# Cached forget gates loaded 64 keys to a partition and summed there, their sums stored once, in a hybrid encoder step on one core

## The chip, the cores and the metric

The kernel runs on one core of a Trainium2 chip. The metric is the time of one execution on the device, in microseconds (us); the time of a kernel is the median of its runs. The engines are called as in the profile: PE is TensorE's matmul, PEld its weight load, DVE is VectorE, ACT is ScalarE, POOL is GpSimd, SP is SyncE, which in this kernel issues every DMA.

## What is computed

One inference step of a trunk of one layer. 1024 frames of a new stream (the prompt) and 16 new frames of each of 8 running streams (the decode rows; each has 1024 past keys in a cache) go through the same layer: RMSNorm, one input projection, three groups of token mixers side by side (stick-breaking attention "sb", a state-space group "ssd", forgetting attention "fox"; 4 heads of 64 in each attention group), one output projection, cross-attention and a SwiGLU FFN. The change concerns the forgetting attention. Its scores have a bias made of running sums of log forget gates:

```python
logf = jax.nn.log_sigmoid((fg + p['fox_b_f']).astype(jnp.float32))   # new rows, 4 heads
...
# prompt: fcum = jnp.cumsum(logf, axis=1)
# decode rows, for each stream:
fcum = jnp.cumsum(jnp.concatenate([past['fox_logf'].astype(jnp.float32), logf], axis=1), axis=1)
fox_o = fox_attend(fq, fox_k, fox_v, fcum[:, past_len:], fcum, qpos, kpos)

def fox_attend(q, k, v, fq, fk, q_pos, k_pos):
    s = jnp.einsum('bqhd,bkhd->bhqk', q, k).astype(jnp.float32) * (HEAD_DIM ** -0.5)
    s = s + (fq[..., :, None] - fk[..., None, :])          # heads moved to the front
    valid = k_pos[None, :] <= q_pos[:, None]
    p = jax.nn.softmax(jnp.where(valid, s, -jnp.inf), axis=-1)
    return jnp.einsum('bhqk,bkhd->bqhd', p, v.astype(jnp.float32))
```

`past['fox_logf']` is the input `cache_fox_logf` with the shape [1, 8 streams, 1024 keys, 4 heads]: 8192 rows of four floats, 0.13 MB. The new `logf` are outputs too (`p_fox_logf` of the prompt, `s_fox_logf` of the decode rows).

## The kernel before

Large products are fp32 in three fp32r products: each operand is split into a high part (`wh`, cast by ACT at L290) and a low part (`wl`, the rest, subtracted at L132 on POOL or DVE), and L326, L327, L328 multiply high by high, low by high and high by low. Tiles come from pools whose names the profile shows: `psd`, `pss`, `pst`, `pso` are PSUM banks for dense products, scores, transposes and outputs of attention; `wr` is a raw piece of a weight or of a cache, `wh` and `wl` its two parts; `ws` a row of scores or weights, `xc` a wide row, `sg` and `so` small scratch tiles, `act` and `st` larger ones, `vr` raw cached values.

The order of the instructions on each engine is set by a scheduler that simulates the program, so the position in the code is a priority, not a place. SP carries all DMAs in one queue of instructions; an SP instruction whose buffer is not free yet stops those behind it.

After the first projections the program is one long pipeline. It steps through units of attention, first those of the sb group, then those of the fox group, and after each unit's step takes one step of a generator of dense work, `fill_s()`: the projections of the fox group's q, k and v, then `fox_sums()`, then z0, dt, xbc and z1, then the ssd group. A prompt unit computes scores of 128 queries (L559, L560, with a mask at L562), turns them into a row of weights (for sb: sigmoids L516 and L517 on ACT and a scan over the row, L519, on DVE; for fox: the bias L529 on ACT, then the exponential) and later multiplies the row by v after transposing it (L577, L592). A decode unit `p` (of four in each group) treats 128 query rows at once, 2 streams of 4 heads of 16 rows. Its cached keys are loaded (L882, two streams by two halves of 512 keys, each in two pieces), transposed on PE (L888, result to PSUM `pst`), multiplied (L873); its weights are multiplied by a reversed product on POOL (L132), transposed on PE (L925) and multiplied by cached values loaded at L943. In the fox group, ACT first writes the bias of all 1024 past keys at L529 from a tile `fkb` that holds, for each of the 128 rows, the 1024 sums of its stream and head (`xc<-fssc`, loaded at L909), and from `fqs`, the sum at the query's own position (loaded at L1246).

`fox_sums()` (L658 to L727) makes these sums. It stores the new gates (L662, L663), loads the cached ones (L666), and builds two masks on POOL: `triu`, a triangle of ones, and `ones`. The prompt's sums are a triangle product and a product with ones (L678, L679) over blocks of 128 rows, transposed (L690) and stored to DRAM as `fcsc` (L692). The cached gates come 128 keys to a column:

```python
SP.dma_start(out=pl0[:, :256].rearrange("p (u h) -> p u h", h=4),
             in_=a["cache_fox_logf"][0].rearrange("b k h -> (b k) h").rearrange("(u p) h -> p u h", p=P))
```

so that partition `p` holds key `p` of each of 64 blocks. They are regrouped (L683), the sums of whole blocks are added up on DVE (L693, L696), and fifteen products on PE (L708 with the triangle, L710 with ones) give 32 rows (8 streams by 4 heads) of 1024 sums in PSUM, copied by ACT. The 16 new rows of each stream follow with a product by `fold` (L713), a scan (L716) and the addition of the last past sum. All of it goes to DRAM twice, `fssc[32, 2, 1040]`, and L909 reads from there, for a unit `p`, 8 rows in 2 copies, each 8 times, in one DMA of 128 partitions.

Of the kernel before, what the change touches and what calls it, by code (L numbers as in the profile page):

```python
# [17 lines left out]
P = 128  # L18
# [3 lines left out]
DEC_B = 8  # L22
# [40 lines left out]
def tile_hybrid_step(ctx: ExitStack, tc: tile.TileContext, a: dict):  # L63
# [37 lines left out]
    def sg_t(dt=F32):  # L101
        return sgp.tile([P, 512], dt, tag="sg", name="sg")
# [128 lines left out]
    def dram(shape, dt, name):  # L231
        return dr.tile(shape, dt, name=name, tag=name)
# [8 lines left out]
    fs_sc = dram([32, 2, PAST + DEC_S], F32, "fssc")  # L241
# [416 lines left out]
    def fox_sums():  # L658
# [6 lines left out]
        pl0, pl1 = sg_t(), sg_t()  # L665
        SP.dma_start(out=pl0[:, :256].rearrange("p (u h) -> p u h", h=4),  # L666
                     in_=a["cache_fox_logf"][0].rearrange("b k h -> (b k) h").rearrange("(u p) h -> p u h", p=P))
        triu, ones = pl1[:, 256:384], pl1[:, 384:512]
        POOL.memset(pl1[:, 256:], 1.0)
# [11 lines left out]

        pp, ps_ = pl1[:, :256], pl0[:, 256:]
        DVE.tensor_copy(pp.rearrange("p (k b h) -> p k b h", k=8, h=4),  # L683
                        pl0[:, :256].rearrange("p (b k h) -> p k b h", k=8, h=4))
# [8 lines left out]
        DVE.tensor_copy(ps_[:, 32:64], pp[:, 0:32])  # L693
# [3 lines left out]
        x8 = sg2_t()  # L697
        DVE.tensor_tensor(out=x8[:, :32].rearrange("p (b h) -> p b h", h=4),
                          in0=lf[:, 8, :].unsqueeze(1).to_broadcast([P, 8, 4]),
                          in1=smask.unsqueeze(2).to_broadcast([P, 8, 4]), op=ALU.mult)  # L700
        yield

        sr = xc_t()[0:32, :PAST + DEC_S]
        for hf in range(2):
            tp = pd()
            for k in range(4 * hf, 4 * hf + 4):
                o = tp[:32, (k % 4) * P:(k % 4 + 1) * P]
                PE.matmul(o, pp[:, k * 32:(k + 1) * 32], triu, start=True, stop=k == 0)  # L708
# [1318 lines left out]
```

## Time and profile before

| | |
|---|---|
| runs | 1922.89, 1914.52, 1916.93 us; median 1916.93 |
| profiled execution | 1915.89 us, its span 1914.2 us |
| busy share of the span | PE 96%, PEld 86%, DVE 47%, ACT 43%, POOL 33% |
| DMA | 305.70 MB in 309742 packets, mean 160 GB/s |
| mean granted TensorE clock | 0.988 |

How to read the lines that follow. A row of windows gives a stretch, its length, then for PE, PEld, DVE, ACT and POOL the busy time with the number of instructions that start in it, the granted TensorE clock as a part of full speed, the mean busy share of the 16 DMA engines (it can pass 1 where transfers overlap on an engine) and the rate in GB/s. A row of the timeline gives the start, the duration, the engine (SPq: SP's queue), line, operation, output and input with their shapes and a count, and in brackets the idle time before it with what ended it. A row of waits gives the waiting engine, tile and line, what it waited for, the total, the number and the longest. Numbers behind tile names are left out there.

### The profile page before, as it was taken

To read this page: it belongs to the slowest core of one execution; us is meant where nothing else is said; L and a number is where in the kernel's file an instruction comes from. 1 tells how busy PE (TensorE), PEld (TensorE's weight loads), DVE (VectorE), ACT (ScalarE), POOL (GpSimd) and SP (SyncE) were. 2 spreads that over 40 slices of the span, in tenths; PEclk is the share of its full clock that TensorE was granted. 3 is DMA by queue.
4 is the path that set the end of the run, shared out by engine and by line. 5 is a ranking of instruction groups with operands and counts; after the bars stand their busy time and mean duration, and the time that the engine had idled before them with its cause. 6 is when DMAs were issued, how large, how long until landed. Compare 5 with 4: busy or idle time off the path is not lost. (4 is left out here: it accounts for less than half of the span.)

```text
span 1914.2 us, 32508 instructions
## 1 busy us (share of the span) xinstructions
PE 1837.6 (96%) x12146; PEld 1641.4 (86%) x12146; DVE 897.1 (47%) x1823; ACT 823.7 (43%) x1782; POOL 622.6 (33%) x921
## 2 busy tenths in 40 slices
PE   7989989999998889999999999999999999999998
PEld 5889877888876667898998889999999999888886
DVE  3421323457646873353445387333333433455554
ACT  6431534545566771243433275333333333344443
POOL 7532416254324563211102205544444443000000
PEclk9999998999999999999999999999999999999999
DMA  9455645536579887244558124322323223567572
GB/s 336 142 165 159 211 115 152 154 109 185 166 220 282 280 290 260 103 150 145 176 194 291 66 91 111 80 70 70 95 74 75 70 70 100 190 194 237 177 246 92
DMA packets 309742, 305.70 MB, mean 160 GB/s; under 512 B 89996, under 2 KB 261108, under 8 KB 309584
## 3 DMA queue, kind: packets, MB, share of 16 engines
q1 hardware_dynamic: 309584, 303.62, 51.6%
q8 instruction: 96, 1.57, 0.3%
q14 instruction: 62, 0.51, 0.1%
HBM read 229.31 MB, written 74.24 MB: 159 GB/s over the span
## 5 line engine op out<-in xcount | busy, mean ns | idle before, releaser
L132 POOL TENSOR_TENSOR wl<-wr,wh 128x256 fp32r<-128x256 f32 (+2 forms) x184 | 138.6, 787 | 222.4 <-ACT wh L290 202.0
L326 PE MATMUL psd<-act,wh 128*128 128x384 f32 x576 | 198.7, 345 | 5.1 <-DVE sg L453 2.7
L327 PE MATMUL psd<-act,wh 128*128 128x384 f32 x576 | 197.6, 343 | 0.0
L328 PE MATMUL psd<-act,wl 128*128 128x384 f32 x576 | 196.8, 342 | 0.7 <-POOL wl L132 0.7
L1849 PE MATMUL pst<-bT,tr 128*128 128x256 f32 (+1 forms) x1068 | 155.0, 293 | 0.0
L1849 PEld LDWEIGHTS pst<-bT,tr 128*128 128x128 f32 x1068 | 144.9, 188 | 0.1
L328 PE MATMUL psd<-wh,act 128*128 128x512 f32 (+3 forms) x424 | 135.8, 322 | 0.0
L326 PE MATMUL psd<-wh,act 128*128 128x256 f32 (+3 forms) x414 | 133.0, 324 | 2.4 <-ACT pt L1445 1.2
L1849 PE MATMUL psd<-bT,tr 128*128 128x320 f32 (+1 forms) x912 | 133.2, 295 | 0.8 <-DVE tr L1693 0.5
L327 PE MATMUL psd<-wl,act 128*128 128x256 f32 (+3 forms) x414 | 132.8, 322 | 0.5 <-POOL wl L132 0.5
L1849 PEld LDWEIGHTS psd<-bT,tr 128*128 128x128 f32 x912 | 124.7, 188 | 1.8 <-DVE tr L1693 0.7
L326 PEld LDWEIGHTS psd<-act,wh 128*128 128x128 f32 x576 | 109.1, 189 | 8.7 <-DVE sg L453 3.1
L132 POOL TENSOR_TENSOR tr<-u,tr 128x256 fp32r<-128x256 f32 x110 | 81.9, 774 | 102.3 <-ACT tr L1689 85.1
L328 PEld LDWEIGHTS psd<-act,wl 128*128 128x128 f32 x576 | 108.9, 189 | 2.3 <-POOL wl L132 1.0
L327 PEld LDWEIGHTS psd<-act,wh 128*128 128x128 f32 x576 | 109.0, 189 | 1.5 <-issue 1.1
L132 POOL TENSOR_TENSOR ws<-ws 128x256 f32<-128x256 f32 (+2 forms) x100 | 68.5, 713 | 115.3 <-DVE ws L519 99.9
L1824 DVE TENSOR_TENSOR tr<-tr,pst 128x256 f32<-128x256 f32 (+1 forms) x86 | 38.6, 449 | 139.5 <-ACT tr L1821 106.3
L251 POOL TENSOR_SCALAR sm<-sm 128x1 f32<-128x1 f32 (+2 forms) x27 | 7.1, 261 | 296.6 <-ACT y L1932 208.0
L132 POOL TENSOR_TENSOR tr<-raw,tr 128x256 fp32r<-128x256 f32 x94 | 69.2, 765 | 84.5 <-ACT tr L1689 76.3
L1689 ACT CAST tr<-tr 128x384 fp32r<-128x384 f32 (+1 forms) x70 | 37.7, 538 | 121.1 <-DMA tr<-hidsc 104.3
L290 ACT CAST wh<-wr 128x512 fp32r<-128x512 f32 (+2 forms) x90 | 52.2, 621 | 80.7 <-PE psd L328 31.0
L326 PEld LDWEIGHTS psd<-wh,act 128*128 128x128 f32 x414 | 78.3, 189 | 9.9 <-ACT pt L1445 1.5
(620 smaller groups left out, 4714.0 us busy)
## 6 DMA issues: line engine op xcount, KB each, us to landing
u<-w_down SPq DMA_DIRECT2D x40, 512.0 KB
raw<-w_down SPq DMA_DIRECT2D x26, 512.0 KB
st<-qksc SPq DMA_DIRECT2D x48, 256.0 KB
wr<-w_in SPq DMA_DIRECT2D x44, 256.0 KB
tr<-hidsc SPq DMA_DIRECT2D x57, 192.0 KB
hidsc<-tr SPq DMA_DIRECT2D x34, 288.0 KB
qksc<-sg SPq DMA_DIRECT2D x48, 192.0 KB
wr<-cache_sb_k SPq DMA_DIRECT2D x32, 256.0 KB
```

Of the source, the lines that this page charges most:

```text
L132: POOL.tensor_tensor(out=out[:, a0:a1], in0=in0[:, a0:a1], in1=in1[:, a0:a1], op=op)
L251: POOL.tensor_scalar(v, ss, inv, EPS, ALU.mult, ALU.add)
L290: ACT.copy(hi, raw)
L326: PE.matmul(out, ah, bh, start=start, stop=False)
L327: PE.matmul(out, ah, bl, start=False, stop=False)
L328: PE.matmul(out, al, bh, start=False, stop=stop)
L1689: ACT.copy(hi, src)
L1824: DVE.tensor_tensor(out=at(out, g), in0=at(x, g), in1=ps[g][:, :GW[g]], op=op)
L1849: PE.matmul(dst[g][:, :GW[g]], x[:, ka], y[:, k, :], start=start and k == 0 and m == 0, stop=stop and k == 3 and m == 2, skip_group_check= ...
```

## The change

The cached gates are loaded as they lie in memory: 64 keys of a stream, each with 4 heads, make 1 KB, and 128 partitions take the 8192 keys (partition = stream x 16 + chunk of 64 keys). On each partition four scans on DVE (one for each head, stride 4 in, dense out) make the running sums of the 64 keys. The last sum of each chunk (`tot`) goes through one product with a mask `before` (ones where the chunk belongs to the same stream and comes earlier), and the result, one number for each partition and head, is added to the 64 sums. The fifteen products and the sums of blocks are gone. The totals of the streams come from a product of `t8` with a column of ones (L710), and are added to the scan of the new rows. The sums are stored once, `fssc[4 heads, 8 streams, 1024]` (L719), the new rows' sums apart in `fnsc[32, 16]` (L721). A unit's `fkb` tile is now loaded by two DMAs (L913), one for each of its two streams: 64 partitions, 4 rows of 1024 sums, each 16 times. `fqs` is loaded from `fnsc` (L1249).

```diff
-    fs_sc = dram([32, 2, PAST + DEC_S], F32, "fssc")
+    fs_sc = dram([4, DEC_B, PAST], F32, "fssc")
+    fn_sc = dram([32, DEC_S], F32, "fnsc")
...
-        pl0, pl1 = sg_t(), sg_t()
-        SP.dma_start(out=pl0[:, :256].rearrange("p (u h) -> p u h", h=4),
-                     in_=a["cache_fox_logf"][0].rearrange("b k h -> (b k) h").rearrange("(u p) h -> p u h", p=P))
-        triu, ones = pl1[:, 256:384], pl1[:, 384:512]
+        lp, tri = sg_t(), sg_t()
+        SP.dma_start(out=lp[:, :256], in_=a["cache_fox_logf"][0].rearrange("b (c k) h -> (b c) (k h)", k=64))
+        triu, ones, before = (tri[:, i * P:(i + 1) * P] for i in range(3))
...
+        b3 = before.rearrange("p (b t) -> p b t", t=16)
+        POOL.affine_select(out=b3, in_=b3, compare_op=ALU.is_ge, fill=0.0, base=-1, pattern=[[16, 8], [1, 16]],
+                           channel_multiplier=-1)
+        POOL.affine_select(out=b3, in_=b3, compare_op=ALU.is_ge, fill=0.0, base=0, pattern=[[-16, 8], [0, 16]],
+                           channel_multiplier=1)
...
-        DVE.tensor_copy(pp.rearrange("p (k b h) -> p k b h", k=8, h=4),
-                        pl0[:, :256].rearrange("p (b k h) -> p k b h", k=8, h=4))
...
-        for k in range(1, 7):
-            sl = slice(32 * k, 32 * k + 32)
-            DVE.tensor_tensor(out=ps_[:, 32 * k + 32:32 * k + 64], in0=ps_[:, sl], in1=pp[:, sl], op=ALU.add)
+        for hd in range(4):
+            x = lp[:, hd:256:4]
+            DVE.tensor_tensor_scan(lp[:, 256 + 64 * hd:320 + 64 * hd], x, x, 0.0, ALU.add, ALU.bypass)
+        tot = pre[:, 32:36]
+        DVE.tensor_copy(tot, lp[:, 319:512:64])
...
-        for hf in range(2):
-            tp = pd()
-            for k in range(4 * hf, 4 * hf + 4):
-                o = tp[:32, (k % 4) * P:(k % 4 + 1) * P]
-                PE.matmul(o, pp[:, k * 32:(k + 1) * 32], triu, start=True, stop=k == 0)
-                if k:
-                    PE.matmul(o, ps_[:, k * 32:(k + 1) * 32], ones, start=False, stop=True)
-            ACT.copy(sr[:, hf * 512:(hf + 1) * 512], tp[:32])
         tp = pd()
-        PE.matmul(tp[:32, :16], x8[:, :32], fold, start=True, stop=True)
+        PE.matmul(tp[:, :4], before, tot, start=True, stop=True)
+        PE.matmul(tp[:32, 16:32], x8, fold, start=True, stop=True)
+        PE.matmul(tp[:32, 32:48], t8, ones[:, :16], start=True, stop=True)
+        DVE.tensor_tensor(out=lp[:, 256:512].rearrange("p (h k) -> p h k", h=4),
+                          in0=lp[:, 256:512].rearrange("p (h k) -> p h k", h=4),
+                          in1=tp[:, 0:4].unsqueeze(2).to_broadcast([P, 4, 64]), op=ALU.add)
...
-        SP.dma_start(out=fs_sc, in_=sr.unsqueeze(1).to_broadcast([32, 2, PAST + DEC_S]))
+        SP.dma_start(out=fs_sc.rearrange("h b (c k) -> (b c) h k", k=64),
+                     in_=lp[:, 256:512].rearrange("p (h k) -> p h k", h=4))
+        SP.dma_start(out=fn_sc, in_=n8)
...
-            SP.dma_start(out=fkb[:, :PAST],
-                         in_=fs_sc[8 * p:8 * p + 8, :, :PAST].rearrange("i c k -> (i c) k").unsqueeze(1)
-                         .to_broadcast([16, DEC_S // 2, PAST]))
+            for b2 in range(2):
+                SP.dma_start(out=fkb[64 * b2:64 * b2 + 64, :PAST],
+                             in_=fs_sc[:, 2 * p + b2, :].unsqueeze(1).to_broadcast([4, DEC_S, PAST]))
```

Line numbers behind the changed function shift by three or four: L882 becomes L885, L888 L891, L909 L913, L925 L928; those ahead of it by one (L315 becomes L316). Only two places of the program are put in another order: the one around `fox_sums`, and the one where `fkb` is loaded.

SP's queue around the load of the cached gates, before. The names are the tile, its number and where the data come from; p_fox_logf and s_fox_logf are the stores of new gates, w_in the weights of the z projection:

```order
L666 DMA sg_2949<-cache_fox_logf 128x64x4
L882 DMA wr_3017<-cache_sb_k 128x512
L882 DMA wr_3019<-cache_sb_k 128x512
L608 DMA mixsc_199<-sg_2921 64x2x256
L882 DMA wr_3034<-cache_sb_k 128x512
L882 DMA wr_3036<-cache_sb_k 128x512
L662 DMA p_fox_logf<-lf_192 128x8x4
L663 DMA s_fox_logf<-lf_192 128x4
L315 DMA wr_3218<-w_in 128x2x256
L315 DMA wr_3218<-w_in 128x2x8
```

SP's queue at the same place, after:

```order
L668 DMA sg_2950<-cache_fox_logf 128x256
L885 DMA wr_3019<-cache_sb_k 128x512
L885 DMA wr_3021<-cache_sb_k 128x512
L609 DMA mixsc_199<-sg_2922 64x2x256
L885 DMA wr_3036<-cache_sb_k 128x512
L885 DMA wr_3038<-cache_sb_k 128x512
L316 DMA wr_3202<-w_in 128x2x256
L316 DMA wr_3202<-w_in 128x2x8
L316 DMA wr_3203<-w_in 128x2x256
L316 DMA wr_3203<-w_in 128x2x8
L316 DMA wr_3218<-w_in 128x2x256
L316 DMA wr_3218<-w_in 128x2x8
```

The order up to the key loads is the same; the two stores of new gates, which stood ahead of the w_in loads, now stand behind six of them.

PE from the first cached keys of this decode unit on, before (L888 transposes keys, L873 multiplies them, L577 transposes weights of a prompt unit, L678 and L679 are the prompt's sums, L690 their transposes):

```order
L873 MATMUL pss<-kf,st 32x512 x4
L888 MATMUL pst<-ident,wr 128x128 x8
L678 MATMUL psd<-lf,sg 128x32
L888 MATMUL pst<-ident,wr 128x128 x4
L679 MATMUL psd<-so,sg 128x28
L888 MATMUL pst<-ident,wr 128x128 x4
L577 MATMUL pst<-ident,ws 128x128 x4
L690 MATMUL psd<-ident,fqc 4x128 x8
L577 MATMUL pst<-ident,ws 128x128 x4
L873 MATMUL pss<-kf,st 32x512 x4
L577 MATMUL pst<-ident,ws 128x128 x3
```

PE at the same place, after:

```order
L876 MATMUL pss<-kf,st 32x512 x4
L891 MATMUL pst<-ident,wr 128x128 x13
L578 MATMUL pst<-ident,ws 128x128 x4
L891 MATMUL pst<-ident,wr 128x128 x3
L578 MATMUL pst<-ident,ws 128x128 x4
L685 MATMUL psd<-lf,sg 128x32
L578 MATMUL pst<-ident,ws 128x128 x3
L876 MATMUL pss<-kf,st 32x512 x4
L904 MATMUL pss<-dm,identr 128x128
L905 MATMUL pss<-st 32x128 x4
L593 MATMUL pso<-pt,st 64x256 x4
L686 MATMUL psd<-so,sg 128x28
```

The triangle product of the prompt's sums (L678, now L685) has moved from the middle of the key transposes to behind them, and the product with ones (L679, now L686) further back still. The join of the chunks stands later on PE, ahead of the first transposes of the decode weights (L925 before, L928 now):

```order
L560 MATMUL pss<-st 128x512
L561 MATMUL pss<-st 128x512
L708 MATMUL psd<-so,sg 128x4
L709 MATMUL psd<-fold,so 32x16
L710 MATMUL psd<-sg,so 32x16
L560 MATMUL pss<-st 128x512
L561 MATMUL pss<-st 128x512
L563 MATMUL pss<-mask_sb,identr 128x128
L928 MATMUL pst<-ident,ws 128x128 x4
```

Here the three small products stand between pieces of 512 keys of a prompt unit, where before the fifteen products with 32 rows stood ahead of such pieces and the product with `fold` alone behind them.

DVE at this place, before (`lf` is the tile of new gates, L402 to L410 compute their logarithm):

```order
L450 TENSOR_TENSOR sg<-so,sg 64x256
L402 TENSOR_SCALAR sg<-sg 128x36
L403 RECIPROCAL sg<-sg 128x36
L404 TENSOR_TENSOR sg<-sg 128x36
L405 TENSOR_TENSOR sg<-sg 128x36
L406 TENSOR_SCALAR sg<-sg 128x36
```

DVE at the same place, after (the scans are listed as SCALAR_TENSOR_TENSOR):

```order
L451 TENSOR_TENSOR sg<-so,sg 64x256
L699 SCALAR_TENSOR_TENSOR sg<-sg 128x64 x4
L403 TENSOR_SCALAR sg<-sg 128x36
L701 COPY so<-sg 128x4
L404 RECIPROCAL sg<-sg 128x36
L704 TENSOR_TENSOR so<-so,smask 128x32
L405 TENSOR_TENSOR sg<-sg 128x36
```

The four scans, which read the loaded gates, now stand ahead of the logarithm of the new gates.

More of the change, by code (lines that the diff above doesn't have):

```diff
@@ L713, in fox_sums @@
-        PE.matmul(tp[:32, :16], x8[:, :32], fold, start=True, stop=True)
-        ACT.copy(x8[0:32, 64:80], tp[:32, :16])
-        n8 = x8[0:32, 64:80]
+        for hd in range(4):
[3 more added lines that the diff above has]
+        DVE.tensor_copy(tot, lp[:, 319:512:64])
+        x8, t8 = pre[:, 64:96], pre[:, 96:128]
+        for out, src in ((x8, lf[:, 8, :]), (t8, tot)):
+            DVE.tensor_tensor(out=out.rearrange("p (b h) -> p b h", h=4), in0=src.unsqueeze(1).to_broadcast([P, 8, 4]),
+                              in1=smask.unsqueeze(2).to_broadcast([P, 8, 4]), op=ALU.mult)
@@ L716, in fox_sums @@
+        n8 = pre[0:32, 128:144]
+        DVE.tensor_copy(n8, tp[:32, 16:32])
         DVE.tensor_tensor_scan(n8, n8, n8, 0.0, ALU.add, ALU.bypass)
[L717 to L718 removed]
+        DVE.tensor_tensor(out=n8, in0=n8, in1=tp[:32, 32:48], op=ALU.add)
+        SP.dma_start(out=fs_sc.rearrange("h b (c k) -> (b c) h k", k=64),
+                     in_=lp[:, 256:512].rearrange("p (h k) -> p h k", h=4))
```

14 lines of the change are left out of this document (3 added, 11 removed).

## The prediction

> **What bounds the kernel now.** I read the page's busy times first, then the busy time of each engine by stretch, then TensorE's waits in the stretch that holds the changed code, then that stretch in order of time.
>
> ```profile
> PE 1837.6 (96%) x12146; PEld 1641.4 (86%) x12146; DVE 897.1 (47%) x1823; ACT 823.7 (43%) x1782; POOL 622.6 (33%) x921
> ```
>
> TensorE is busy for 96% of the span, so a change pays only where it takes TensorE work away or closes one of its gaps. By stretch (columns: stretch, its length, busy time of PE, PEld, DVE, ACT, POOL with instructions, granted TensorE clock, DMA share, GB/s):
>
> ```profile
> 200.00:276.00 76.00, 72.84 (x575) 63.64 (x574) 23.24 (x36) 34.92 (x82) 25.73 (x44) 0.98 0.56 171
> 276.00:312.00 36.00, 25.63 (x167) 20.16 (x166) 14.92 (x43) 19.29 (x45) 19.55 (x31) 0.76 0.75 165
> 312.00:400.00 88.00, 85.94 (x714) 76.25 (x715) 42.91 (x78) 40.16 (x96) 40.51 (x58) 1.00 0.49 141
> ...
> 500.00:600.00 100.00, 93.11 (x707) 77.46 (x706) 56.15 (x176) 58.06 (x131) 22.04 (x40) 0.98 0.80 227
> 600.00:700.00 100.00, 86.60 (x717) 66.86 (x716) 81.43 (x226) 76.32 (x174) 61.91 (x104) 0.97 0.84 266
> ```
>
> The forget-gate sums run from 276 to 312, and there TensorE is idle for 10.4 of 36 us, at a mean clock of 0.76. TensorE's own waits from 250 to 340 (total, times, longest):
>
> ```profile
> PE pst L888 <- DMA wr<-cache_sb_k: 5.5, 3, 4.9
> PE pst L925 <- POOL ws L132: 3.5, 1, 3.5
> ```
>
> The same place in order of time, from two windows:
>
> ```profile
> 276.99 0.45 SPq L666 DMA_DIRECT2D sg<-cache_fox_logf  x1
> 277.54 5.25 SPq L882 DMA_DIRECT2D wr<-cache_sb_k  x2
> 283.56 1.02 SPq L882 DMA_DIRECT2D wr<-cache_sb_k  x2
> 284.20 0.29 DVE L683 COPY sg<-sg 128x256 f32<-128x256 f32 x1 [1.11 <-DMA sg<-cache_fox_logf]
> 285.00 1.51 PE L888 MATMUL pst<-ident,wr 128*128 128x128 f32 x6 [4.91 <-DMA wr<-cache_sb_k]
> ...
> 286.12 5.14 SPq L315 DMA_DIRECT2D wr<-w_in  x8
> 287.52 1.09 PE L888 MATMUL pst<-ident,wr 128*128 128x128 f32 x4 [0.32 <-DMA wr<-cache_sb_k]
> 292.48 0.63 ACT L290 CAST wh<-wr 128x528 fp32r<-128x528 f32 x1 [1.66 <-DMA wr<-w_in]
> 293.20 8.52 POOL L132 TENSOR_TENSOR wl<-wr,wh 128x256 fp32r<-128x256 f32 x12 [9.76 <-PE pst L577]
> 297.77 2.56 DVE L519 TENSOR_TENSOR_SCAN ws<-ws 128x1152 f32<-128x1152 f32 x1 [8.67 <-ACT ws L516]
> 301.72 3.56 POOL L132 TENSOR_TENSOR ws<-ws 128x256 f32<-128x256 f32 x3
> 304.73 0.49 PE L925 MATMUL pst<-ident,ws 128*128 128x128 f32 x1 [3.50 <-POOL ws L132]
> ```
>
> Read it from the top. The load of cached gates is issued at 276.99 and its data are there at 284.2, 7.2 us later. The key loads behind it stand in SP's queue for 5.25 us, and TensorE waits 4.91 us for them. What that load is, the transfers from 277 to 285 tell:
>
> ```profile
> DMA packets 8811, 0.95 MB, mean 118 GB/s; under 512 B 8270, under 2 KB 8555, under 8 KB 8811
> ```
>
> 8270 of 8811 packets are under 512 B: 128 partitions x 64 rows of four floats are 8192 pieces of 16 B. The 0.13 MB of this load therefore hold up everything behind them. The second wait is the end of a chain that starts with the same delay: the w_in loads are issued from 286.12 on, cast at 292.48, split by POOL from 293.20 to 301.72, and only then does POOL multiply the decode weights that L925 transposes at 304.73. The gaps cost a second time in the clock (same columns as above):
>
> ```profile
> 282.00:284.00 2.00, 0.00 (x0) 0.00 (x0) 0.95 (x5) 0.00 (x0) 0.60 (x2) 0.57 1.08 115
> 290.00:292.00 2.00, 2.00 (x11) 1.49 (x11) 0.00 (x0) 0.58 (x1) 0.00 (x0) 0.50 0.34 61
> 302.00:304.00 2.00, 0.00 (x0) 0.00 (x0) 2.00 (x2) 0.37 (x2) 2.00 (x1) 0.69 1.10 301
> 308.00:310.00 2.00, 2.00 (x15) 1.88 (x13) 0.10 (x1) 2.00 (x6) 2.00 (x5) 0.60 0.87 218
> ```
>
> **The change, part by part.** All sums are against the profiled execution, 1915.9 us with its span of 1914.2; the median of the runs shown is 1916.93, 1.0 above it.
>
> *The load in rows of 1 KB.* 128 pieces take the place of 8192, so the key loads are no longer held. SP issues the four of them and the one store between at about 0.5 us each from 277.54, so all are issued by about 280, and the first landing is near where TensorE falls idle now (285.00 less 4.91 is 280.1). I count the 4.9 us as closed, but for about 0.5 us at the last two key loads.
>
> *What is late next.* The first w_in load goes into a buffer that the first key transposes free, at about 280.6 instead of 286.12: 5.5 us earlier. From issue to cast takes 6.36 us now (292.48 less 286.12). In the new order the two stores of new gates no longer stand ahead of these loads; for the key loads issued at 283.56, issue to use was 3.96 us (287.52). Between 4.0 and 6.4 I take 4.4, since the stores' 16-byte pieces go as well. The chain then starts 7.5 us earlier; POOL's split (8.5 us) and the 3.0 us from 301.72 to 304.73 stay. L925's successor comes at about 297.2. TensorE is not later than that: of the 16.2 us from 285.0 to the gap at 301.2, 3.3 go with the removed products, 3.6 with the half clock up to about 292 (7.2 us at 0.5), which leaves 9.3 of work after 281.5, or 290.8, and the waits below add 2 to 4.
>
> *New waits there.* Four scans stand on DVE ahead of the sums of the new gates, and behind the load. A scan of 128x64 has no row; the nearest are
>
> ```profile
> L519 DVE TENSOR_TENSOR_SCAN ws<-ws 128x128 f32<-128x128 f32 x4 | 2.7, 663 | 0.6 <-ACT ws L516 0.6
> L716 DVE TENSOR_TENSOR_SCAN so<-so 32x16 f32<-32x16 f32 x1 | 0.6, 556 | 0.0
> ```
>
> so between 0.56 and 0.66 us each; 0.6 gives 2.4 us. With a load back at about 279 the sums of the new gates end near 285.5 instead of 282.7, and the triangle product (L685) waits for them for some 2 us. This lies in the time before L925's successor and costs nothing while the POOL chain is later; without that cover it costs the 2 us.
>
> *Products.* Removed are fifteen matmuls of L708 and L710, which run as 30 halves; added are three small ones, of which two load full columns of 32 or fewer.
>
> ```profile
> L708 PEld LDWEIGHTS psd<-sg x16: 106/110/110, 294.7 to 298.8; 128*32 128x32 f32 x16
> L678 PEld LDWEIGHTS psd<-lf,sg x2: 333/335/337, 286.5 to 286.7; 128*128 128x128 f32 x2
> ```
>
> 30 x 0.11 is 3.3 us less. The join over 128 columns costs 2 x 0.17 (0.335 at half clock), the total of a stream 2 x 0.11; the fold product was there before. Net 2.7 us less TensorE work, inside the same stretch, so it only keeps TensorE ahead of the POOL chain and is not added.
>
> *Behind L925.* Two 512-wide pieces that stood between L925 and the z projection now stand ahead of it, one 256-wide piece has come in, and the wait for the new rows' sums (DVE, behind a long scan) is about as now: 0.5 us less. The stage gives 7.5 + 0.5 = 8 us. Its ends are 4 (the load lands no sooner and a new wait of 1.5 us shows) and 11 (issue to cast 4.0, and full clock after 304.7).
>
> *Small edits.* POOL makes two more masks (L670's kind, 0.29 us) while it has no other work before 293.20; without that cover 0.6 us. The sums' store becomes 512 pieces of 256 B, used 210 us later. The new rows' own store adds one issue. DVE loses the regrouping copy and seven short sums, ACT three copies of sums; both lie ahead of a scan that waits 8.67 us for sigmoids (297.77), so I count nothing.
>
> *The bias loads of the forgetting group.* Each of the four loads of 512 KB becomes two of 256 KB, each reading four rows, sixteen times each. These rows tell when one is issued and used, and how full the DMA engines are:
>
> ```profile
> 520.17 0.68 SPq L909 DMA_DIRECT2D xc<-fssc  x1
> ...
> 529.53 0.54 SPq L909 DMA_DIRECT2D xc<-fssc  x1
> ...
> 525.66 1.15 ACT L529 ACTIVATE ws<-xc,fqs 128x1024 f32<-128x1024 f32 x1 [3.97 <-DMA xc<-fssc]
> 527.41 0.36 ACT L415 ACTIVATE so<-psd 128x256 f32<-128x256 f32 x1
> ...
> 582.50 1.16 ACT L529 ACTIVATE ws<-xc,fqs 128x1024 f32<-128x1024 f32 x1
> 583.69 0.55 SPq L909 DMA_DIRECT2D xc<-fssc  x1
> ...
> 632.72 1.15 ACT L529 ACTIVATE ws<-xc,fqs 128x1024 f32<-128x1024 f32 x1
> ...
> 520.00:530.00 10.00, 10.00 (x82) 9.16 (x81) 4.60 (x12) 5.27 (x13) 4.26 (x12) 1.00 1.04 293
> 540.00:550.00 10.00, 10.00 (x90) 7.68 (x82) 4.11 (x14) 7.13 (x14) 1.54 (x3) 1.00 1.01 317
> ```
>
> Four more issues of 0.55 us cost SP 2.2 us, beside DMA engines that are full anyway. What no row shows is over how many of the 16 DMA engines a load spreads whose source has only four rows. If over all 16: the bytes are the same, cost 0. If over four: at 317 GB/s over 16 engines one moves 19.8 GB/s, so 0.524 MB take 6.6 us over four instead of 1.65, 5 us more for each load, 20 us for four if all of it shows. The first shows: ACT already waits 3.97 us for it, and the z projection behind L415 needs the bank that ACT frees at 527.41. The second is issued at 529.53 and used at 582.50, the third 49 us before its use, so these can only hold up what queues behind them on full engines. I take 7: 3.5 for the first, 1.2 for each of the others. That is nearer the low end, because TensorE shows no idle time from 540 to 550 at full engines. The range keeps 0 and 20.
>
> The Trainium skill (DMA: Bandwidth & Descriptors, section "Why a DMA increments its semaphore by 16 and not by 1") says that a load is spread over the largest number of engines up to 16 that divides the slowest dimension of source and destination. By that, 4 rows onto 64 partitions go to four engines, the high end of the transfer time holds for all four loads, and no run here shows it yet.
>
> Sum: 1915.9 - 8 + 7 = 1914.9, so 1915.
>
> **The rivals.** *Slower.* Place: the four bias loads. If each sits on four engines, every load behind it ends 5 us later on those four. For it: the stretches from 520 to 550 run at a DMA share above 1, and 600 to 700 at 0.84 with TensorE idle 13.4 us. Against it: the loads after the first have some 50 us until use, and TensorE's waits for DMAs from 500 to 700 come to 7.5 us in two rows:
>
> ```profile
> PE psd L1055 <- DMA act<-xbcsc: 5.1, 3, 3.0
> PE pst L888 <- DMA wr<-cache_fox_k: 2.4, 1, 2.4
> ```
>
> All of it exposed gives 1915.9 - 8 + 20 = 1928. It decides from 17.6 us on, since 8 come back and 0.5% of 1916.9 is 9.6. This is the case that the rule above speaks for.
>
> *Faster.* The bias loads spread evenly or hide, cost 0 to 1, and the stage gives 9 to 11 us: 1915.9 - 10.5 = 1905.5. For it: both gaps and both stretches of half clock go back to one load. Against it: DVE's new scans, and POOL's 8.5 us of splitting, which nothing shortens.
>
> *The change does not do what it says.* The key loads could be late for another reason, such as SP's queue waiting on buffers; then only the products go, 2.7 us, and a cost of 1 at the bias loads: 1914. Against it stand the 8270 small packets and L683, which gets their data 0.8 us before TensorE's wait ends.
>
> **How the numbers follow.** The forecast (stage 8, bias loads 7) has 0.62, with its own range from 1908 to 1922. Faster has 0.14, slower 0.12, no effect on the loads 0.12. A measurement of this kernel tells about 0.5% from no change, 9.6 us: below 1907.3 is faster, above 1926.5 slower. Below 1907.3 lie 0.11 of the faster case and 0.02 of the forecast, 0.13; above 1926.5 lie 0.09 of the slower case and 0.01, 0.10; the rest is 0.77. The range of 8 in 10 reaches into both rivals, 1906 to 1925.
>
> **What would show it.** In the new profile TensorE's wait for cache_sb_k near 280 should be under 1.5 us, the 276 to 312 stretch should reach the z projection about 8 us sooner, L925's successor should still wait for POOL, and there should be no 15 products of 32 rows. At 510 to 525 ACT's wait for the bias load tells the second term: about 4 us means an even spread, 7.5 or more the four engines. The prediction is wrong if the stage gives under 4 or over 11, or if TensorE's idle time from 500 to 700, 20.3 us by the page's stretches, grows by more than 12.

## The result, and the profile after

| | before | changed |
|---|---|---|
| median | 1914.78 us (6 runs, 1913.19 to 1922.89) | 1935.77 us (6 runs, 1932.28 to 1939.45) |
| ratio | | 1.0103, 95% interval 1.0082 to 1.0124 |
| profiled execution | 1915.89 us, span 1914.2 us | 1934.31 us, span 1932.3 us |

The change makes the kernel 17 to 21 us slower: measured once more later, beside other runs of the kernel before, it took 1933.84 against 1916.70 us, ratio 1.0085 (1.0072 to 1.0098). The forecast was 1915 with a range up to 1925; the rival called slower, at 1928, was the one that came, and more so.

First the busy times, and the same stretches as before with the one from 400 to 500 (columns as there):

```profile
PE 1843.6 (95%) x12120; PEld 1645.1 (85%) x12120; DVE 892.0 (46%) x1823; ACT 822.5 (43%) x1779; POOL 627.8 (32%) x923
200.00:276.00 76.00, 72.14 (x581) 63.08 (x579) 24.05 (x38) 36.06 (x85) 27.26 (x46) 1.00 0.59 174
276.00:312.00 36.00, 25.61 (x160) 20.41 (x160) 16.70 (x47) 17.88 (x42) 23.86 (x37) 0.81 0.64 161
312.00:400.00 88.00, 84.01 (x696) 73.61 (x696) 41.47 (x73) 40.25 (x95) 40.35 (x53) 1.00 0.50 142
400.00:500.00 100.00, 97.67 (x653) 87.79 (x652) 62.37 (x98) 53.45 (x123) 41.48 (x56) 0.98 0.49 146
500.00:600.00 100.00, 89.15 (x652) 73.42 (x650) 52.38 (x166) 53.37 (x121) 17.83 (x32) 0.91 0.70 197
600.00:700.00 100.00, 84.39 (x679) 65.24 (x676) 67.77 (x195) 66.66 (x152) 56.76 (x92) 0.91 0.77 243
```

TensorE is busy for 6 us more with fewer matmuls. Two things stand out: the forget-gate stretch, 276 to 312, leaves TensorE as idle as before (busy for 25.6 of 36 us in both), and from 500 to 700 the rows count 1331 matmuls (652 and 679) where they counted 1424, at a clock of 0.91 where it was 0.98 and 0.97, while the DMA engines are less busy than before (0.70 and 0.77 against 0.80 and 0.84).

Where the time goes can be told closer. Outside the two places TensorE's matmuls come in the same order in both kernels, so they can be matched one by one; the table says how much later (+) the changed kernel, or an experiment, falls against the profile of before over two stretches. Each row is from one profile.

| kernel | 265 to 340: forget-gate sums | 505 to 760: bias loads |
|---|---|---|
| changed | -0.8 | +17.5 |
| changed, second profile | -3.1 | +18.8 |
| changed, 16 rows to a load | -0.8 | -1.0 |
| changed, 8 rows to a load | -0.5 | +6.4 |
| changed, 4 rows in the first unit only | -1.3 | +7.6 |
| changed, eight loads of one row to a unit | -3.5 | +10.5 |
| before, with loads of 4 rows | -0.6 | +21.0 |
| before, with two loads of 16 rows | -2.3 | -3.0 |

The last two rows have the old sums, so their -0.6 and -2.3 in the first column are what profiles of the same code differ by. The new sums, with -0.5 to -3.5, are not told apart from that. The loss is in the second column, but for some 2 us that fall between the two. From 402 to 406 every profile of the new sums in the table loses 1.6 us again, at a clock of 0.50 that lasts 3.4 us; no profile with the old load of the gates has that. The row from 400 to 500 shows it, 0.98 above against this one of before:

```profile
400.00:500.00 100.00, 97.60 (x666) 87.29 (x663) 64.07 (x101) 54.42 (x126) 42.78 (x59) 1.00 0.52 149
```

Why the clock falls there was not tried.

**The loss.** ACT's wait for the first bias load, TensorE's longest waits from 500 to 760 and the places in order of time, in the changed kernel:

```profile
ACT ws L530 <- DMA xc<-fssc: 10.7, 1, 10.7
PE psd L327 <- DVE sg L417: 6.7, 1, 6.7
PE pst L891 <- DMA wr<-cache_fox_k: 6.1, 1, 6.1
...
520.24 1.20 SPq L913 DMA_DIRECT2D xc<-fssc  x2
532.35 1.15 ACT L530 ACTIVATE ws<-xc,fqs 128x1024 f32<-128x1024 f32 x1 [10.74 <-DMA xc<-fssc]
534.97 0.58 PE L327 MATMUL psd<-wh,act 128*128 128x256 f32 x1 [6.66 <-DVE sg L417]
...
594.05 0.40 SPq L1148 DMA_DIRECT2D s_ssm<-act  x1
594.50 5.25 SPq L913 DMA_DIRECT2D xc<-fssc  x1
599.84 2.35 SPq L885 DMA_DIRECT2D wr<-cache_fox_k  x3
607.47 1.09 PE L891 MATMUL pst<-ident,wr 128*128 128x128 f32 x4 [6.14 <-DMA wr<-cache_fox_k]
```

The first load is issued at 520.24, as before (520.17), but used at 532.35 instead of 525.66. ACT stands still for 10.7 us in front of it. L416 and L417, which take the z projection's result out of PSUM, stand behind it, so TensorE finds no free bank and waits 6.7 us.

At 594.50 a later bias load takes SP itself 5.25 us to issue, where the usual issue takes some 0.55; three loads of cached keys are behind it in SP's queue, and TensorE waits 6.1 us for keys. The long issue is not new. The kernel before has one of 5.18 us at the same place, behind the same store of `s_ssm`, and there it is a load of keys:

```profile
584.33 0.54 SPq L1145 DMA_DIRECT2D s_ssm<-act  x1
584.96 5.18 SPq L882 DMA_DIRECT2D wr<-cache_fox_k  x1
```

What is new is how the loads behind it end. Each DMA engine that carries a load reports when its part is done; these are the trace's completion records. Of the keys issued at 584.96 in the kernel before, all sixteen engines report from 592.41 to 593.85, and TensorE waits 2.4 us. Of those issued at 599.84 in the changed kernel, twelve report from 602.40 to 603.51 and four only from 606.48 to 607.34; TensorE goes on at 607.47.

That only a part of the DMA engines carries the bias loads can be seen in the DMA share (the last column but one):

```profile
529.00:530.00 1.00, 0.00 (x0) 0.00 (x0) 0.00 (x0) 0.00 (x0) 0.00 (x0) 1.00 1.11 365
535.00:536.00 1.00, 1.00 (x5) 1.00 (x6) 0.34 (x2) 0.69 (x3) 0.63 (x1) 0.50 0.26 99
542.00:543.00 1.00, 1.00 (x11) 1.00 (x11) 0.23 (x2) 1.00 (x4) 0.90 (x1) 1.00 0.27 106
```

When the others have run dry the share stands at 0.26 and 0.27, four of sixteen. The completion records agree: the first unit's two loads have four reports each, from 526.36 to 527.45 and from 530.91 to 532.27, where a load over all engines has sixteen. The normalising weights, loaded by the DMA behind it at 522.00, are reported by twelve engines from 529.3 to 529.7 and by the other four at 535.1 to 535.9. So four engines run 6 us behind the rest, and a load that spans all sixteen ends with them.

**The stage of the sums.** Two of TensorE's waits from 250 to 340, and the place in order of time:

```profile
PE pst L928 <- POOL ws L132: 4.9, 1, 4.9
PE pst L891 <- DMA wr<-cache_sb_k: 1.9, 2, 1.4
...
275.27 0.45 SPq L668 DMA_DIRECT2D sg<-cache_fox_logf  x1
277.42 0.86 DVE L699 TENSOR_TENSOR_SCAN sg<-sg 128x64 f32<-128x64 f32 x4 [0.81 <-DMA sg<-cache_fox_logf]
284.09 0.64 ACT L291 CAST wh<-wr 128x528 fp32r<-128x528 f32 x1
284.67 0.46 SPq L663 DMA_DIRECT2D p_fox_logf<-lf  x1
284.81 4.71 POOL L132 TENSOR_TENSOR wl<-wr,wh 128x256 fp32r<-128x256 f32 x9 [2.82 <-ACT wh L291]
285.79 0.43 SPq L316 DMA_DIRECT2D wr<-w_in  x1
290.69 0.63 ACT L291 CAST wh<-wr 128x528 fp32r<-128x528 f32 x1 [2.90 <-DMA wr<-w_in]
291.40 5.56 POOL L132 TENSOR_TENSOR wl<-wr,wh 128x256 fp32r<-128x256 f32 x3 [1.88 <-ACT wh L291]
291.53 3.01 DVE L520 TENSOR_TENSOR_SCAN ws<-ws 128x1152 f32<-128x1152 f32 x1 [2.72 <-ACT ws L517]
296.96 7.56 POOL L132 TENSOR_TENSOR ws<-ws 128x256 f32<-128x256 f32 x9
300.43 1.13 PE L928 MATMUL pst<-ident,ws 128*128 128x128 f32 x4 [4.92 <-POOL ws L132]
305.19 0.57 PE L327 MATMUL psd<-wh,act 128*128 128x264 f32 x1
```

The load of the gates does what was said: 2.15 us from issue to the scan, and TensorE's wait for keys falls from 4.9 us to 1.4 and 0.5. But the wait for POOL at L928 has grown from 3.5 to 4.9 us, and behind it TensorE runs at half clock until about 309:

```profile
302.00:304.00 2.00, 2.00 (x13) 1.93 (x13) 0.98 (x4) 0.57 (x3) 2.00 (x4) 0.50 0.04 8
308.00:310.00 2.00, 2.00 (x15) 2.00 (x14) 0.00 (x0) 0.00 (x0) 1.11 (x4) 0.77 0.00 0
```

The z0 projection begins 5.1 us earlier than before (310.25), of which 1.7 us were there ahead of the changed code (this profile already ran that much ahead at 265), and goes at half speed for its first 3.6 us. The piece of POOL's product that ends just ahead of L928 (297.56 to 300.37) takes 2.82 us beside a third scan on DVE, where five of these nine pieces take 0.63 to 0.64.

### The profile page after: what moved, and what is told of

Same layout as the page of the kernel before. It is cut to its first block, busy times and chain, and to the rows that moved or that the text cites. A ratio compares the mean times of both kernels' runs of the same rounds, so it can differ in the third digit from the quotient of the medians.

```text
span 1932.3 us, 32467 instructions
## 1 busy us (share of the span) xinstructions
PE 1843.6 (95%) x12120; PEld 1645.1 (85%) x12120; DVE 892.0 (46%) x1823; ACT 822.5 (43%) x1779; POOL 627.8 (32%) x923
## 4 chain that ended last, share of the span: by engine, by line
PE 78%; DMA 8%; POOL 5%; issue 4%; ACT 2%; DVE 2%; SPq 1%; POOLq 0%; DVEq 0%; ACTq 0%
PE psd L1852 10%; PE psd L327 10%; PE psd L328 9%; PE psd L329 9%; PE pst L1852 8%; PE pss L1852 3%; PE pss L327 3%; PE pss L328 3%; POOL wl L132 3%; PE pss L329 3%; PE pso L1852 2%; PE pso L593 1%; PE pst L327 1%; PE pst L328 1%; PE pst L329 1%
## 5 line engine op out<-in xcount | busy, mean ns | idle before, releaser
L328 PEld LDWEIGHTS psd<-wl,act 128*128 128x128 f32 x414 | 80.1, 194 | 8.7 <-issue 2.1
```

Source lines behind the costliest of these rows:

```text
L328: PE.matmul(out, ah, bl, start=False, stop=False)
```

## The experiments

The theory after this reading, A: a load is spread over as many DMA engines as the slowest dimension of its source has rows; four rows put every bias load on four engines, and that is the whole loss. Rivals: two DMAs in the place of one, with the order around them (B); the stores (C); the new stage, which shifts the phase of all that follows (D).

### The rows of the bias loads: 16 and 8 in the place of 4

```diff
-    fs_sc = dram([4, DEC_B, PAST], F32, "fssc")
+    fs_sc = dram([4, 4, DEC_B, PAST], F32, "fssc")
...
-        SP.dma_start(out=fs_sc.rearrange("h b (c k) -> (b c) h k", k=64),
-                     in_=lp[:, 256:512].rearrange("p (h k) -> p h k", h=4))
+        for x in range(4):
+            SP.dma_start(out=fs_sc[:, x].rearrange("h b (c k) -> (b c) h k", k=64),
+                         in_=lp[:, 256:512].rearrange("p (h k) -> p h k", h=4))
...
-                             in_=fs_sc[:, 2 * p + b2, :].unsqueeze(1).to_broadcast([4, DEC_S, PAST]))
+                             in_=fs_sc[:, :, 2 * p + b2, :].rearrange("h x k -> (h x) k").unsqueeze(1).to_broadcast([16, DEC_S // 4, PAST]))
```

> The changed kernel, but the sums are stored four times ([4 heads, 4 copies, 8 streams, 1024]), so that each of the two bias loads of a unit reads 16 rows four times instead of 4 rows sixteen times; the order of the instructions stays, with three more stores. Theory A (a load runs over as many DMA engines as its source has rows, and four rows put 0.26 MB on four of the 16 engines): ACT's wait for the first bias load falls from 10.7 us to about 4, the 18 us that TensorE loses between 510 and 660 come back, and the kernel takes 1914 to 1919 us. Theory B (the loss comes from two DMAs in the place of one and from the order around them): 1930 or more, and ACT's wait stays near 10. Theory C (the extra stores of 0.13 MB near 300 us matter): TensorE falls behind already at 300 to 320.

Measured: 1911.85 us, ratio to the kernel before 0.9968 (0.9954 to 0.9982), 2 us under A's range. Theory C falls: up to 340 the extra stores cost nothing (-0.8, as without them). With two copies in the place of four:

> As with four copies, but two copies, so each bias load reads 8 rows eight times. Theory A (engines by rows): 0.52 MB over eight engines instead of four; the time beyond an even spread falls from 5 us for a unit to 1.65, a third, so about 6 of the 18 us stay: 1921 us, between the changed kernel and the one with 16 rows. Theory B (two DMAs, order): 1930 or more, as the changed kernel. If it were a threshold (any spread under 16 engines costs in full): 1930 too, while 16 rows come back to 1917.

Measured: 1922.04 us, ratio 1.0021 (1.0006 to 1.0035). ACT's wait for the first load, with 16 rows and then with 8, both with the order of the changed kernel:

```profile
ACT ws L530 <- DMA xc<-fssc: 4.6, 1, 4.6
...
ACT ws L530 <- DMA xc<-fssc: 6.4, 1, 6.4
```

Four, eight and sixteen rows give waits of 10.7, 6.4 and 4.6 us and times of 1934 to 1936, 1922 and 1912 us: a dose and its response, with nothing else changed but one to three more stores of 0.13 MB. Theory B, which left both at 1930, falls, and so does a threshold. TensorE's share of the stretch says the same (first the kernel before, then the changed one, then 16 rows):

```profile
500.00:760.00 260.00, 237.55 (x1803) 188.41 (x1802) 165.79 (x461) 153.46 (x344) 111.72 (x183) 0.98 0.83 258
...
500.00:760.00 260.00, 228.88 (x1725) 180.44 (x1724) 157.63 (x454) 150.10 (x339) 105.69 (x175) 0.93 0.79 247
...
500.00:760.00 260.00, 238.62 (x1810) 188.07 (x1807) 165.42 (x464) 154.58 (x348) 111.98 (x184) 0.99 0.81 258
```

### The loads alone, on the old sums

```diff
-            SP.dma_start(out=fkb[:, :PAST],
-                         in_=fs_sc[8 * p:8 * p + 8, :, :PAST].rearrange("i c k -> (i c) k").unsqueeze(1)
-                         .to_broadcast([16, DEC_S // 2, PAST]))
+            for b2 in range(2):
+                SP.dma_start(out=fkb[64 * b2:64 * b2 + 64, :PAST],
+                             in_=fs_sc[8 * p + 4 * b2:8 * p + 4 * b2 + 4, 0, :PAST].unsqueeze(1).to_broadcast([4, DEC_S, PAST]))
```

> The kernel before with the load of the biases alone changed: two DMAs for a unit, each of four rows sixteen times; the sums themselves are made as before. Theory A: the loss is all in these loads, so 1915 plus 18 is 1933 us, and ACT's wait at the first load is about 10 us. Rival D (the loss comes from the new forget-gate stage, which puts the later loads into a worse phase): 1915 to 1920.

Measured: 1934.01 us, ratio 1.0094 (1.0069 to 1.0118); ACT's wait is 11.6 us. The loads by themselves bring the whole loss; rival D falls. The same two loads with 16 rows, from sums that are stored four times:

```diff
-    fs_sc = dram([32, 2, PAST + DEC_S], F32, "fssc")
+    fs_sc = dram([32, 4, PAST + DEC_S], F32, "fssc")
...
+                SP.dma_start(out=fkb[64 * b2:64 * b2 + 64, :PAST], in_=fs_sc[8 * p + 4 * b2:8 * p + 4 * b2 + 4, :, :PAST]
+                             .rearrange("i c k -> (i c) k").unsqueeze(1).to_broadcast([16, DEC_S // 4, PAST]))
```

> The sums of the kernel before, stored four times, and two bias loads for a unit, each of 16 rows four times. Its order is that of the kernel before with the four-row loads, so the pair differs in the rows alone; and against the changed kernel with four copies it differs in the sums alone. Theory A: the four-row loads cost the same on the old sums, so this takes 16 to 20 us less than the 1934 of that one: 1914 to 1918 us. If the new sums bring the 6 us by which the changed kernel with four copies is under the kernel before, this one stays at the time of the kernel before, 1916 to 1919; if the two loads in the place of one bring it (each can be used on its own queue place), this one too is at 1911 to 1913.

Measured: 1914.97 us, ratio 0.9989 (0.9974 to 1.0003). Against the four-row loads it gains 19 us with the same order of instructions. ACT's wait, four rows and then sixteen:

```profile
ACT ws L529 <- DMA xc<-fssc: 11.6, 1, 11.6
...
ACT ws L529 <- DMA xc<-fssc: 3.4, 1, 3.4
```

The new sums with the same loads were at 0.9968, the old ones at 0.9989; the intervals overlap, so the 4 us between the ratios are not settled as a gain of the new sums. The changed kernel was run once more beside it:

> The changed kernel itself once more, beside the kernel before on one chip, with a second profile. All theories: 1.0 to 1.1% over the kernel before, 1934 to 1938 us. It serves to tell how far the 6 us of the new sums, which the comparison of the two kernels with 16 rows shows, are there with four rows too: if they add, the changed kernel is 6 us under the kernel before with four-row loads, 1928; if not, it is at 1934 or over.

Measured: 1933.84 us, ratio 1.0085 (1.0072 to 1.0098). With four-row loads the new sums are level with the old (1934.01). The 6 us of the expectation are not there.

### Which load costs what

The kernel with four copies, but the first unit's two loads read four rows (`fs_sc[:, 0, 2 * p + b2, :]`, repeated 16 times, where `p == 0`).

> The kernel with four copies, but the bias loads of the first decode unit of the forgetting group read four rows sixteen times, as in the changed kernel; the other three units' loads keep 16 rows. The order of the instructions is the same. It sizes the prediction's two terms. If the first load alone shows its delay and the others are mostly hidden (the prediction's 3.5 and 1.2 each): 1912 plus 3.5 to 8 is 1915 to 1920. If the delay of four busy engines goes on to the loads behind it and into later units whatever they read: 1912 plus 10 or more. The trace of the changed kernel shows TensorE 8 us later at 530 and 10 us more between 560 and 660, so the reading is 8 and 10.

Measured: 1920.70 us, ratio 1.0016 (1.0003 to 1.0028), with waits of ACT for the load, and of TensorE for the bank:

```profile
ACT ws L530 <- DMA xc<-fssc: 10.1, 1, 10.1
PE psd L327 <- DVE sg L417: 6.0, 1, 6.0
```

The first unit's loads cost 9 us (1920.70 less 1911.85), the other three units' together 13 to 15 (1933.84 or 1935.77 less 1920.70). Its runs lie between the two expectations, nearer to the lower one; that the delay goes on into later units whatever they read is not shown. But the loads of the other units are not hidden either.

### Rows or the slowest dimension

Eight loads for a unit, each of one row sixteen times, from sums stored once: the source has one row, but its slowest dimension, the repeats, has sixteen steps.

```diff
-            for b2 in range(2):
-                SP.dma_start(out=fkb[64 * b2:64 * b2 + 64, :PAST],
-                             in_=fs_sc[:, 2 * p + b2, :].unsqueeze(1).to_broadcast([4, DEC_S, PAST]))
+            for r in range(8):
+                SP.dma_start(out=fkb[16 * r:16 * r + 16, :PAST],
+                             in_=fs_sc[r % 4, 2 * p + r // 4, :].unsqueeze(0).to_broadcast([DEC_S, PAST]))
```

> The changed kernel (sums stored once), with eight bias loads for a unit in the place of two: each of one row, sixteen times, onto 16 partitions. Theory A1 (the number of engines is that of the slowest dimension of source and destination, which is here the sixteen repeats): each load runs over 16 engines, ACT's wait at the first is about 4 to 6 us plus up to 3.3 for six more issues, and the kernel takes 1915 to 1925 us. Theory A2 (it is the number of different rows in memory): each load runs on one engine; eight of 64 KB on one to eight engines cost more than four rows on four: 1936 or more.

Measured: 1930.12 us, ratio 1.0065 (1.0046 to 1.0085). The 32 loads and ACT's wait for the first unit's:

```profile
L913 SPq DMA_DIRECT2D xc<-fssc x32: 303/418/3651, 518.1 to 635.4; - x32
DMA to landing us min/median/max: 2.4/3.0/3.4
ACT ws L530 <- DMA xc<-fssc: 1.6, 1, 1.6
```

On the spread, A1 is right: ACT waits 1.6 us, less than in any other kernel here, and the completion records of these loads show sixteen engines each. On the total both theories missed. The scheduler puts the 32 loads, and what it had around them, in another order from 520 on, and against the kernel with 16 rows TensorE falls back by 15 us between 531 and 685; which of the moved instructions does it was not tried.

### The stage: the load, the stores and POOL

The load of the gates alone, in the kernel before (the products then read gates in the wrong order, so the decode sums are not the reference's):

```diff
-        SP.dma_start(out=pl0[:, :256].rearrange("p (u h) -> p u h", h=4),
-                     in_=a["cache_fox_logf"][0].rearrange("b k h -> (b k) h").rearrange("(u p) h -> p u h", p=P))
+        SP.dma_start(out=pl0[:, :256],
+                     in_=a["cache_fox_logf"][0].rearrange("b (c k) h -> (b c) (k h)", k=64))
```

> The kernel before with the load of the cached gates alone changed to 64 keys to a partition (1 KB pieces); the products that follow read them as if they lay in the old order, so the decode sums are not the reference's. Theory E (the stage gives back what the load frees: with the gate stores now ahead of the last piece of w_in, POOL's split of it comes late, and L925 waits for POOL as long as before): TensorE's wait of 4.9 us at L888 goes, but the kernel gains 0 to 3 us: 1912 to 1915. Theory F (the prediction's stage sum): 7 to 8 us, 1907.

Measured: 1918.56 us, ratio 1.0001 (0.9983 to 1.0020). Neither 1907 nor even 1912 to 1915: no change that can be told, though the longest wait for keys falls from 4.9 to 2.1 us:

```profile
PE pst L888 <- DMA wr<-cache_sb_k: 2.4, 2, 2.1
```

In its profile the z0 projection begins 4.0 us earlier than in the kernel before, counted from 265, and at 450 TensorE is 2.4 us behind. The load also changes the order from the stage on, so this says that it is worth nothing by itself here, not why. TensorE does not wait for POOL at L925, so theory E's reason is not the one here.

For the why, the two stores of new gates were moved behind the stage (a copy of `lf` made after L728 is stored in its place), in the kernel with four copies:

> The kernel with four copies, and the two stores of new gates (1152 pieces of 16 B) moved from SP's queue ahead of the last piece of w_in to behind the forget-gate stage, by way of a small copy on DVE. Theory E (these stores hold up the last pieces of w_in, ACT casts them at 290.7 instead of 287.3, POOL's last three splits then fall under DVE's scans and take 5.6 us instead of 2.1, and L928 waits for POOL 4.9 us): the cast comes 3 us earlier, TensorE's wait for POOL falls to 1 to 3 us, and the kernel takes 2 to 5 us less than with four copies alone: 1907 to 1910 where that one takes 1912. Theory G (the stage ends with POOL whatever the stores do): the wait stays at 4 to 5 us and the time within 1 us.

Measured: 1911.37 us, ratio 0.9979 (0.9964 to 0.9993): the same as without, so theory E's 1907 to 1910 does not come. In its profile TensorE gains 2.4 us between 260 and 320 on the kernel with four copies; ACT waits 0.6 us for the last piece of w_in where it waited 3.2, but TensorE's wait for POOL stays, because the last of the twelve pieces still fall under DVE's scans:

```profile
PE pst L928 <- POOL ws L132: 5.4, 1, 5.4
296.47 0.63 ACT L291 CAST wh<-wr 128x528 fp32r<-128x528 f32 x1 [0.61 <-DMA wr<-w_in]
293.90 10.23 POOL L132 TENSOR_TENSOR wl<-wr,wh 128x256 fp32r<-128x256 f32 x12 [3.29 <-ACT wh L291]
298.28 2.56 DVE L520 TENSOR_TENSOR_SCAN ws<-ws 128x1152 f32<-128x1152 f32 x1 [0.51 <-ACT ws L517]
```

Then the split of z0's weights was put on DVE (`eng=DVE` in `w_unit` for z0), alone and with the stores:

> The kernel with four copies, and the low parts of the z0 weights subtracted on DVE (four of 528 columns, some 0.6 us each) instead of on POOL (twelve pieces, three of which took 5.6 us beside DVE's scans). Theory H (POOL is what L928 waits for, because its pieces stand still while DVE scans): POOL is free when the scan of the decode weights ends, TensorE's wait at L928 falls from 4.9 us to 1 to 3 us, and z0 begins 2 to 4 us earlier; the whole takes 1908 to 1911 us where four copies alone take 1912, if the order behind it, which changes from 305 us on, costs nothing. Theory G (the scan on DVE and the three pieces of the product set the end, whoever splits): the wait stays above 4 us.

> Both: the stores of new gates behind the stage, and the low parts of the z0 weights on DVE. If the two causes add up (2.4 us came back in the trace from the stores alone, where TensorE still waits 5.4 us for POOL): z0 begins 4 to 6 us earlier than with four copies alone, and the kernel takes 1906 to 1910 us. If they are the same microseconds: no more than with the split on DVE alone.

Measured: 1919.39 us, ratio 1.0014 (1.0000 to 1.0029), and 1915.51 us, ratio 0.9993 (0.9979 to 1.0006). The total of TensorE's waits for POOL, alone and then with the stores (total, times, longest):

```profile
PE pst L928 <- POOL ws L132: 2.8, 2, 2.2
...
PE pst L928 <- POOL ws L132: 3.0, 3, 1.7
```

The wait falls from 4.9 to 2.2 and 1.7 us, as H says. With both, z0 begins 4.2 us earlier than with four copies alone, counted from 265 in each profile. But the order behind it changes, and at 450 TensorE is 1.1 us behind. Neither is faster; both times lie over what H and the sum of the two causes said. So POOL under the scans is what L928 waits for, and what closing that wait gains is given back later; by what was not settled.

The kernel with four copies, with or without the two stores moved, is the one that beats the kernel before by more than its interval (0.9954 to 0.9982 without), and it beats the changed one by 22 to 24 us.

## Why the prediction was wrong

**The bias loads, +7.** The mechanism was named, with both ends, and the choice between them was the step that failed. Taken was 7, "nearer the low end, because TensorE shows no idle time from 540 to 550 at full engines"; measured, from 16 rows to 4, are 19 to 24 us, over the high end of 20. Three things were undersized.
- The first load was put at 3.5 of a 5 us longer transfer. ACT's wait grew by 6.7 us (10.7 less 3.97). The reports of the two halves come one behind the other, the second 4.8 us after the first; from that 0.26 MB over four engines are an estimated 14 GB/s for each engine, where the sum had taken 19.8. TensorE lost 6.7 us in one wait and then ran on half clock (0.54 from 530 to 540). The first unit costs 9.
- The other three were put at 1.2 each, since they have some 50 us until their use. They cost 13 to 15 together. ACT does not wait for them; what is late is queued behind them. The one place that was followed is the load of keys issued at 599.84: its last four engines report 3.8 us behind the other twelve, and TensorE waits 6.1 us instead of 2.4. "These can only hold up what queues behind them" was right, and it was priced at 1.2 each.
- The row taken as the tie-breaker, no idle time at full engines, says nothing of four engines: the mean share over sixteen does not tell how far the slowest four are behind.

The Trainium skill (DMA: Bandwidth & Descriptors, section "Why a DMA increments its semaphore by 16 and not by 1") had spoken for the high end; sixteen, eight and four rows, and one row with sixteen repeats, agree with its rule of the slowest dimension. The Trainium skill says in the same section that it is the lowest-numbered of the engines, which would put all eight half loads on the same four; that the first two end one behind the other fits that, and no run here shows which engines they are.

**The stage, -8.** Every step up to ACT held: the keys' wait fell under 1.5 us, and the first w_in piece was cast 8.4 us earlier (284.09 for 292.48; 7.5 were forecast, and 1.7 of the 8.4 were there before). The step that failed is "POOL's split (8.5 us) and the 3.0 us ... stay". That the two stores of new gates no longer stood ahead of the w_in loads was counted as a gain; they now stand ahead of the last piece, which is cast at 290.69, 6.6 us behind the first. POOL waits 1.9 us for it, and two of its last three pieces then stand under DVE's scans, so that the three take 5.56 us. From the first cast to the transpose there were 12.25 us before (292.48 to 304.73) and are 16.34 now, so L925's successor came at 300.43, not at 297.2. TensorE was ahead of it, as forecast, but that made its idle time 4.9 us, behind which the z0 projection ran at half clock. In the place of 8 us the matched matmuls show 0.8 and 3.1 up to 340, nothing that can be told from the scatter of the old sums, and 1.6 of it is lost again at 402 to 406.

**The checks.** The wait for keys, POOL as the end of the stage and the fifteen products came as said. The wait of ACT was to tell four engines from sixteen at 7.5 us; it was 10.7. One check was badly made: TensorE's idle time from 500 to 700 was to grow by more than 12 us if the forecast was wrong. It grew by 6.2 (20.3 to 26.5), because matmuls at half clock count as busy; matched matmuls, +17.5 us, say it rightly.

**The chances.** The rival slower was worked out with its place, its price and a rule that speaks for it, and got 0.12. The evidence against it, 50 us until use, was about the loads themselves and not about those behind them. (The sum of the faster case comes to 1905.4, not 1905.5, which changes nothing.)

## What to carry to other kernels

Before a DMA is made from fewer rows, count over how many engines it will be spread: a broadcast load of four rows ran at a quarter of the width, and storing a small tensor four times, 0.5 MB in all, was worth 22 to 24 us over storing it once. When the DMA engines are full, price such a load by what is queued behind it, not by the slack until its own use. And where a wait ahead of a join is closed, look for the last piece of the other branch, not the first: here the stage ended with POOL either way.

## What the hardware showed beside that

A piece on POOL can stand still while DVE scans. The twelve splits of z0's weights in the changed kernel (shortest, median, longest in ns):

```profile
L132 POOL TENSOR_TENSOR wl<-wr,wh x12: 222/728/2983, 284.8 to 295.0; 128x256 fp32r<-128x256 f32 x8, 128x16 fp32r<-128x16 f32 x4
```

The first nine (three of them of 16 columns) take 4.71 us while DVE scans nothing, the last three (one of 16 columns) 5.56 us; the longest piece, 2.98 us, starts at 292.08 and ends at 295.06, 0.5 us behind the scan of 1152 columns beside it (291.53 to 294.54). The scan is late too: it starts while a piece on POOL has 0.59 us to go and takes 3.01 us, where the same scan in the kernel before has 0.12 us of a piece to sit out and takes 2.56. The Trainium skill (SBUF — State Buffer, section "SBUF: two separate sides") says that DVE and GpSimd share one pair of ports as a lock, which whichever starts first holds for the whole instruction; among DVE's instructions it names those with two inputs from SBUF, against a GpSimd instruction that reads SBUF. This scan names two such inputs, and the trace agrees.

An issue of a DMA can hold SP itself. In all thirteen profiles of this case the issue behind each of the two `s_ssm` stores (2048 pieces of 512 B each) takes 2.9 to 5.3 us, whatever it loads or stores, where the usual one takes some 0.55. No run here shows what it waits for.
